# A DiT block on one core: a gate moved into the S5 readout, the widest pooling sums beside the chunk states, and stores spread over two queues

## The chip, the core and the metric

The kernel runs on one core of one Trainium2 chip. The metric is the device time of one execution in microseconds. Engines are named as the profile names them: PE is TensorE (matmuls), DVE is VectorE, ACT is ScalarE, SP is SyncE, which only issues DMAs here. ACT also issues DMAs from its own queue (ACTq).

## The reference

One layer over 1024 latent tokens of width 1024, with 256 context tokens that seed the scans. Cut to what matters:

```
sh1, sc1, g1, sh2, sc2, g2 = split(silu(c) @ w_mod + b_mod, 6)
h  = rms_norm(x, norm1_g) * (1 + sc1) + sh1
hc = (the same of ctx, modulated from c_ctx)
u_a, u_b, gate_a, gate_b = split(h @ w_in)         # 512, 512, 1024, 1024 columns
st_f, st_b = s5_states(u_a, both directions, seeded with the last state of hc @ w_in)
y   = gelu(real(c_f @ st_f + c_b @ st_b) + d_skip * u_a)
y_a = (y * sigmoid(y @ w_glu + b_glu)) @ w_branch_a
y_b = concat_j((mean over a window of 2, 4, 8, 16 in a row of 64 - u_b) @ pool_w[j]) * pool_scale @ w_branch_b
x   = x + g1 * ((sigmoid(gate_a) * y_a + sigmoid(gate_b) * y_b) @ w_out)
h2  = rms_norm(x, norm2_g) * (1 + sc2) + sh2
x   = x + g2 * ((silu(h2 @ w_gate) * (h2 @ w_up)) @ w_ffn_out)
out = rms_norm(x, final_norm_g)
```

## The kernel before, in words

Every product of float32 numbers is made in three passes (`mm3`, lines 264, 266 and 268): both operands are split into a rounded high part (`hi`) and a rest (`lo`), and hi·hi, hi·lo and lo·hi are summed in PSUM. ACT makes the high part of a weight tile (line 97), DVE the rest (line 98); `W8.take(ahead)` hands out the next tile and prepares as many behind it as `ahead` says, in the order of `weight_order`. Activations lie as 8 tiles of 128 features by 1024 tokens; one projection of 128 output columns (`proj`) is 8 k-steps of 6 matmuls of 128x512, so 48.

The kernel sets its own order: each engine runs its instructions in the order in which the code writes them, and a queue that waits holds all that stands behind it. Generators called `side` put other work between the k-steps of a projection. The stages:

- `startup`: c through w_mod (`mod_rows` multiplies two 512 KB `wm` tiles, which `load_mod` loads on SP), norm of x, transposes (`trans`), and the first three pooling columns (`mm`, into `self.ub`).
- `input_proj`: six projections. Beside them `build_e` makes the matrices E (16 steps, `ET`), `build_f` the matrices F (16 steps: DVE makes a tile `ef` in three operations, it is stored as `Fd`, and eight small matmuls with it give `kb`, stored as `Md`), and `pool_diff` the pooling branch of the windows j = 0 to 3: running sums by doubling (line 860), times the inverse width (line 867), minus the input (line 870), stored as `dT[j]`.
- `chunk_states`: U and ET tiles are loaded, and ET·U (line 1214) gives the states `V[0]` and `V[1]` of both directions, d = 0 and 1. Ahead of these products stands the gate b1. Then `scan_steps` on DVE (lines 1258 to 1261) beside the gates b2 to b7 and a0 to a3.
- readout: `f_phase(m)`, m = 0 to 3, 96 matmuls of 128x128 each (lines 1339 and 1341) with the loads `Fw`, `M` and `U` of `f_loads`; ACT applies gelu (line 1343) into `y`, and eight DMAs store it as `yT`. A gate is one projection with a sigmoid (line 1316), stored as `siga` or `sigb`.
- `late_gates`: the gates a4 to a7; between their k-steps the `yT` and `dT` tiles come back and are split (`tiles`), and w_mod's other sections are multiplied (`sections`). `pool_mm` applies pool_w. `branches`: four glu products, then both branches; output projection, FFN.

Of the kernel before, what the change touches and what calls it, by code (L numbers as in the profile page):

```python
# [11 lines left out]
F32 = mybir.dt.float32  # L12
# [223 lines left out]
class Kernel:  # L236
# [81 lines left out]
    def run(self):  # L318
# [36 lines left out]
        with self.pool("fpool", side="right") as fp:  # L355
            loads = [self.f_loads(fp, m) for m in range(2)]
            self.gate("a", 0, 4, side)
            for _ in side:
                pass
            for m in range(4):  # L360
                self.f_phase(fp, m, loads)
        par.close()
# [12 lines left out]
    def weight_order(self):  # L375
        W = self.W8 = Weights(self)
        cols = lambda w, c, n: w[:, c:c + n].rearrange("(k p) m -> p k m", p=128)
        two = [(0, 0), (0, 128)]
        w_in = self.w_in[0]
        W.units += W.job([cols(w_in, 896, 128)], 8, 128, [(0, 0)])  # L380
        for c in list(range(0, 512, 256)) + list(range(2048, 3072, 256)) + list(range(1024, 2048, 256)):
            W.units += W.job([cols(w_in, c, 256)], 8, 256, two)
            if c == 1280:
                W.units += W.job([self.pool_w[0].rearrange("j c m -> c j m")], 4, 128, [(0, 0)])
# [89 lines left out]
    def startup(self, hs):  # L474
# [168 lines left out]
        mm(0, 0)  # L643
        mm(1, 0)
# [9 lines left out]
        mod_rows(1)  # L654
        load_mod(2, 0)
        load_mod(2, 1)
# [96 lines left out]
    def input_proj(self):  # L753
# [6 lines left out]
        pools = [self.pool_diff(sp, j) for j in range(4)]  # L760
# [11 lines left out]
        def pool_steps():  # L772
            for j in range(4):
                next(pools[j])
                yield
                if 1 <= j <= 2:
                    begin(j + 1, self.ub[j + 1])
                yield from pools[j]

        pooling = pool_steps()  # L780
        for kt, q in ((6, 1), (7, 0), (7, 1)):
            self.mm_ub(kt, q)
            next(mats)
            self.drain(5)
# [27 lines left out]
        self.ub.append(self.proj(None, side))  # L812
# [9 lines left out]
        self.gate("b", 0, 1, side)  # L822
# [19 lines left out]
    def pool_diff(self, ep, j):  # L842
# [5 lines left out]
        up = ep.tile([128, 80, 16], F32, name="up", bufs=2)  # L848
# [7 lines left out]
        while True:  # L856
            a, b = (1, 0) if width == 2 else (width // 4, width // 4)
            s = ep.tile([128, 80, 16], F32, name="s", bufs=3)
            n = hi - b - lo - a
            G.tensor_tensor(s[:, lo + a:lo + a + n], cur[:, lo:lo + n], cur[:, lo + a + b:lo + a + b + n], op=OP.add)  # L860
            cur, lo, hi = s, lo + a, hi - b
            yield
            if width == w:
                break
            width *= 2
        d = cur[:, 8:72]
        G.tensor_tensor(d, d, self.inv[:, j, :, None].to_broadcast([128, 64, 16]), op=OP.mult)
        yield
        dn = ep.tile([128, 80, 16], F32, name="s", bufs=3)[:, 0:64].rearrange("p r s -> p (r s)")
        G.tensor_tensor(dn.rearrange("p (t b i) -> p i t b", t=8, b=16), d.rearrange("p (i t) b -> p i t b", t=8),  # L870
                        up[:, 8:72].rearrange("p (i t) b -> p i t b", t=8), op=OP.subtract)
# [314 lines left out]
    def chunk_states(self, es):  # L1186
# [21 lines left out]
        self.gate("b", 1, 2)  # L1208
# [121 lines left out]
    def f_phase(self, fp, m, loads):  # L1330
        nc = self.nc
        Fw, M, U = loads[m]
        y = fp.tile([128, 8, 128], F32, name="y")
# [13 lines left out]
        for t in range(8):  # L1347
            nc.sync.dma_start(self.yT[m][:, t].rearrange("(g c) n -> c g n", c=16), y[t * 16:t * 16 + 16])
# [95 lines left out]
    def late_gates(self):  # L1444
# [5 lines left out]
        def tiles():  # L1450

            srcs = []
            for kind, j in todo:
                for q in range(2):
                    srcs.append((kind, j, q, self.dT[j][:, q * 512:q * 512 + 512] if kind == "d" else
                                 self.yT[j][:, q * 4:q * 4 + 4].rearrange("p t n -> p (t n)")))
# [21 lines left out]
        def side(n, m):  # L1478
            for i in range(8):
                if i % 2 == 0 and i // 2 < n:  # L1480
                    next(tiles, None)
                elif m > 3 or i > 5:
                    next(sections, None)
# [11 lines left out]
    def branch(self, acts, left, side=None):  # L1495
        wh, wl = self.W8.take(min(2, left))
        ps = [self.psum() for _ in range(2)]
        for k in range(4):
            self.mm3(ps, wh[:, k], wl[:, k], acts[k], k == 0, k == 3)
            if side and k % 2:  # L1500
# [3 lines left out]
    def branches(self):  # L1504
        nc = self.nc

        ya = []
        for m in range(4):
            ps = self.branch(self.ys, 2, self.sections)
            ts = []  # L1510
            for q in range(2):
                t, u = self.ld(), self.ld()
                nc.scalar.activation(t, ps[q], AF.Sigmoid, bias=self.cols[:, 84 + m:85 + m])
                hi, lo = self.ys[m][q]
                nc.vector.tensor_tensor(u, hi.bitcast(F32), lo.bitcast(F32), op=OP.add)
                nc.vector.tensor_tensor(t, t, u, op=OP.mult)
                ts.append(t)
# [585 lines left out]
```

## Time and profile before

| what | value |
| --- | --- |
| median of 3 runs | 1316.56 us (1312.87 to 1317.75) |
| profiled execution | 1315.17 us, its span 1313.4 us |
| PE busy | 1246.1 us (95%) |
| DVE busy | 948.5 us (72%) |
| ACT busy | 531.4 us (40%) |
| mean granted clock of PE | 0.988 of full speed |
| HBM traffic | 182 GB/s over the span |

Times in the trace count from the start of the span. Busy time is that of the engine's instructions; idle time is put down to what ended it. `<-` reads "written from" in a row's names and "released by" in its brackets. The granted clock is a share of full speed: 0.50 is the lower of TensorE's two levels, 1.2 GHz, 1.00 the upper, 2.4 GHz.

### The profile page before, as it was taken

To read this page: it belongs to the slowest core of one execution; us is meant where nothing else is said; L and a number is where in the kernel's file an instruction comes from. 1 tells how busy PE (TensorE), PEld (TensorE's weight loads), DVE (VectorE), ACT (ScalarE), POOL (GpSimd) and SP (SyncE) were. 2 spreads that over 40 slices of the span, in tenths; PEclk is the share of its full clock that TensorE was granted. 3 is DMA by queue.
4 is the path that set the end of the run, shared out by engine and by line. 5 is a ranking of instruction groups with operands and counts; after the bars stand their busy time and mean duration, and the time that the engine had idled before them with its cause. 6 is when DMAs were issued, how large, how long until landed. Compare 5 with 4: busy or idle time off the path is not lost.

```text
span 1313.4 us, 16704 instructions
## 1 busy us (share of the span) xinstructions
PE 1246.1 (95%) x5811; PEld 1005.1 (77%) x5811; DVE 948.5 (72%) x1778; ACT 531.4 (40%) x951; POOL 13.4 (1%) x36
## 2 busy tenths in 40 slices
PE   6888989999969999999999999999999999999996
PEld 4567757878868788788887788888888888888884
DVE  7779983899606696855679977678778766578576
ACT  5564214742225521222574333333333345454443
POOL 4000000000000000000000000000000000000000
PEclk8999999999989999999999999999999999999998
DMA  8624569126477665653514733676666539776543
GB/s 286 182 97 162 180 184 339 65 81 216 145 183 251 208 211 189 209 175 111 199 35 141 235 107 108 147 233 206 227 209 203 175 126 321 272 227 194 189 144 129
DMA packets 196428, 239.79 MB, mean 183 GB/s; under 512 B 16928, under 2 KB 117880, under 8 KB 195832
## 3 DMA queue, kind: packets, MB, share of 16 engines
q1 hardware_dynamic: 188200, 222.92, 52.8%
q10 hardware_dynamic: 8144, 15.80, 3.2%
q8 instruction: 46, 0.75, 0.2%
q14 instruction: 38, 0.31, 0.1%
HBM read 168.67 MB, written 70.00 MB: 182 GB/s over the span
## 4 chain that ended last, share of the span: by engine, by line
PE 59%; DVE 19%; DMA 9%; ACT 7%; issue 4%; SPq 1%; ACTq 0%; DVEq 0%
PE ps L1724 10%; PE ps L1722 10%; PE ps L1723 9%; PE ps L1953 5%; PE ps L1954 5%; PE ps L1952 5%; PE ps L268 2%; PE ps L264 2%; PE ps L266 2%; PE ps L1568 2%; PE ps L1566 2%; PE ps L1567 2%; DMA wm<-in_w_mod_dram 1%; DVE wt L98 1%; DMA Md<-kb 1%
## 5 line engine op out<-in xcount | busy, mean ns | idle before, releaser
L1722 PE MATMUL ps<-a,wt 128*128 128x512 f32 x436 | 172.7, 396 | 2.4 <-ACT ld L1836 2.4
L1724 PE MATMUL ps<-a,wt 128*128 128x512 f32 x436 | 171.5, 393 | 0.3 <-DVE wt L124 0.3
L1723 PE MATMUL ps<-a,wt 128*128 128x512 f32 x436 | 170.6, 391 | 0.0
L124 DVE TENSOR_TENSOR a<-a,a 128x512 fp32r<-128x512 f32 x162 | 103.3, 685 | 30.9 <-ACT a L225 30.2
L1953 PE MATMUL ps<-a,a 128*128 128x512 f32 x308 | 122.0, 396 | 1.1 <-DVE a L124 1.1
L1952 PE MATMUL ps<-a,a 128*128 128x512 f32 x308 | 121.8, 396 | 0.0
L1954 PE MATMUL ps<-a,a 128*128 128x512 f32 x308 | 121.8, 396 | 0.0
L264 PE MATMUL ps<-h,wt 128*128 128x512 f32 x336 | 109.0, 405 | 5.1 <-ACT wt L97 4.7
L268 PE MATMUL ps<-h,wt 128*128 128x512 f32 x336 | 105.4, 395 | 2.0 <-DVE wt L98 1.9
L266 PE MATMUL ps<-h,wt 128*128 128x512 f32 x336 | 105.0, 394 | 0.0
L225 ACT ACTIVATE a<-a 128x512 fp32r<-128x512 f32 x154 | 87.1, 624 | 42.9 <-DVE a L124 13.2
L1722 PEld LDWEIGHTS ps<-a,wt 128*128 128x128 f32 x436 | 81.8, 188 | 21.1 <-ACT ld L1836 3.3
L1724 PEld LDWEIGHTS ps<-a,wt 128*128 128x128 f32 x436 | 81.9, 188 | 20.4 <-DVE wt L124 1.2
L1723 PEld LDWEIGHTS ps<-a,wt 128*128 128x128 f32 x436 | 82.0, 188 | 18.4
L1366 ACT ACTIVATE a<-ld 128x512 fp32r<-128x512 f32 x64 | 39.3, 629 | 128.4 <-DVE ld L1543 64.9
L264 PEld LDWEIGHTS ps<-h,wt 128*128 128x128 f32 x336 | 60.3, 190 | 19.9 <-ACT wt L97 5.7
L268 PEld LDWEIGHTS ps<-h,wt 128*128 128x128 f32 x336 | 60.8, 189 | 16.6 <-DVE wt L98 4.6
L266 PEld LDWEIGHTS ps<-h,wt 128*128 128x128 f32 x336 | 61.7, 190 | 12.5
L98 DVE TENSOR_TENSOR wt<-raw,wt 128x1024 fp32r<-128x1024 f32 (+1 forms) x42 | 39.8, 951 | 43.5 <-ACT wt L97 43.4
L1953 PEld LDWEIGHTS ps<-a,a 128*128 128x128 f32 x308 | 57.9, 188 | 15.8 <-DVE a L124 1.9
L1952 PEld LDWEIGHTS ps<-a,a 128*128 128x128 f32 x308 | 57.9, 188 | 14.0
L1954 PEld LDWEIGHTS ps<-a,a 128*128 128x128 f32 x308 | 57.9, 188 | 13.9
(336 smaller groups left out, 2456.0 us busy)
## 6 DMA issues: line engine op xcount, KB each, us to landing
raw<-in_w_ffn_in_dram SPq DMA_DIRECT2D x44, 512.0 KB
ld<-in_w_mod_dram SPq DMA_DIRECT2D x64, 256.0 KB
a<-in_w_ffn_out_dram SPq DMA_DIRECT2D x55, 256.0 KB
raw<-in_w_in_dram SPq DMA_DIRECT2D x10, 1024.0 KB
wm<-in_w_mod_dram SPq DMA_DIRECT2D x16, 512.0 KB
ld<-in_w_ffn_out_dram SPq DMA_DIRECT2D x22, 256.0 KB
x<-in_x_dram SPq DMA_DIRECT2D x8, 512.0 KB
ETd<-out ACTq DMA_DIRECT2D x16, 256.0 KB
```

Source lines behind the costliest of these rows:

```text
L98: nc.vector.tensor_tensor(lo, src, hi.bitcast(F32), op=OP.subtract)
L124: self.K.nc.vector.tensor_tensor(lo, self.src, hi.bitcast(F32), op=OP.subtract)
L225: K.nc.scalar.activation(hi, t, AF.Copy)
L264: nc.tensor.matmul(o, wh, ah, start=first, stop=False)
L266: nc.tensor.matmul(o, wh, al, start=False, stop=False)
L268: nc.tensor.matmul(o, wl, ah, start=False, stop=last)
L1722: nc.tensor.matmul(p, wh, ah, start=first and k == 0, stop=False, skip_group_check=on)
L1723: nc.tensor.matmul(p, wh, al, start=False, stop=False, skip_group_check=on)
L1724: nc.tensor.matmul(p, wl, ah, start=False, stop=last and k == 3, skip_group_check=on)
L1952: nc.tensor.matmul(p, ah[:, s], wh, start=first and i == 0, stop=False, skip_group_check=on)
L1953: nc.tensor.matmul(p, ah[:, s], wl, start=False, stop=False, skip_group_check=on)
L1954: nc.tensor.matmul(p, al[:, s], wh, start=False, stop=i == NB - 1, skip_group_check=on)
```

## The change

1. `run`: gate a4 stands between `f_phase` 1 and 2 of the readout; `late_gates` keeps a5 to a7, with five `tiles` and three `sections` beside each, and the fourth `pool_mm` stands behind them. The order of weight tiles follows.
2. `startup`: `mod_rows(1)` and the two `load_mod` behind it stand between `mm(0, 0)` and `mm(1, 0)` rather than behind `mm(0, 1)`.
3. `input_proj`: gate b0 first, in place of the column for pool j = 3 (896), gate b1 last; only three pools.
4. `pool_diff`: one operation makes sum·(1/w) - u, and two small ones on the first and last eight columns put the edges right.
5. `build_f`: `Fd` is stored by ACT's queue; six `ef` buffers rather than four, three `kb` rather than two.
6. `chunk_states`: the projection of pool j = 3 stands where gate b1 stood, and its sums run on DVE in the room of `V[1]`.
7. `f_phase`: `y` lies in three parts of `work`, used in turn, and its eight stores alternate between ACT and SP.
8. `branches`: y is loaded again from `yT` where DVE added its two parts (line 1515), and four `sections` steps stand beside a glu product, not two.

```diff
@@ run
             for m in range(4):
                 self.f_phase(fp, m, loads)
+                if m == 1:
+                    self.gate("a", 4, 5, None, 2)
@@ startup
         mm(0, 0)
+        mod_rows(1)
+        load_mod(2, 0)
+        load_mod(2, 1)
         mm(1, 0)
...
         mm(0, 1)
-        mod_rows(1)
-        load_mod(2, 0)
-        load_mod(2, 1)
         self.s5_load_b()
@@ input_proj
             self.mm_ub(kt, q)
+            self.drain(8)
             next(mats)
-            self.drain(5)
...
-        self.ub.append(self.proj(None, side))
+        self.gate("b", 0, 1, side)
         for m in range(4):
             ps = self.proj(hc, side)
...
-        self.gate("b", 0, 1, side)
+        self.gate("b", 1, 2, side)
@@ pool_diff
-        d = cur[:, 8:72]
-        G.tensor_tensor(d, d, self.inv[:, j, :, None].to_broadcast([128, 64, 16]), op=OP.mult)
+        dn = new_s()[:, 0:64].rearrange("p r s -> p (r s)")
+        d, u = (x[:, 8:72].rearrange("p (i t) b -> p i t b", t=8) for x in (cur, up))
+        o = dn.rearrange("p (t b i) -> p i t b", t=8, b=16)
+        G.scalar_tensor_tensor(o, d, 1.0 / w, u, op0=OP.mult, op1=OP.subtract)
         yield
-        dn = ep.tile([128, 80, 16], F32, name="s", bufs=3)[:, 0:64].rearrange("p r s -> p (r s)")
-        G.tensor_tensor(dn.rearrange("p (t b i) -> p i t b", t=8, b=16), d.rearrange("p (i t) b -> p i t b", t=8),
-                        up[:, 8:72].rearrange("p (i t) b -> p i t b", t=8), op=OP.subtract)
+
+        d, u, o = (x[:, ::7] for x in (d, u, o))
+        inv = self.inv[:, j].rearrange("p (i t) -> p i t", t=8)[:, ::7]
+        G.tensor_tensor(d, d, inv[:, :, :, None].to_broadcast([128, 2, 8, 16]), op=OP.mult)
+        G.tensor_tensor(o, d, u, op=OP.subtract)
         nc.sync.dma_start(self.dT[j], dn)
@@ ef_tiles
-        return sp.tile([128, 576], F32, name="ef", bufs=4), sp.tile([128, 576], F32, name="eft", bufs=2)
+        return sp.tile([128, 576], F32, name="ef", bufs=6), sp.tile([128, 576], F32, name="eft", bufs=2)
@@ build_f
-                    kb[u] = sp.tile([128, 240], F32, name="kb", bufs=2)
+                    kb[u] = sp.tile([128, 240], F32, name="kb", bufs=3)
...
-                nc.sync.dma_start(self.Fd[bu // 2][:, bd, bu % 2 * 4:bu % 2 * 4 + 4],
+                nc.scalar.dma_start(self.Fd[bu // 2][:, bd, bu % 2 * 4:bu % 2 * 4 + 4],
@@ chunk_states
-        self.gate("b", 1, 2)
+
+        room = V[1].rearrange("p i g b -> p (i g b)")
+        part = [room[:, i * 1280:i * 1280 + 1280].rearrange("p (r b) -> p r b", b=16) for i in (0, 1, 2, 3, 1, 2)]
+        wide = self.pool_diff(3, lambda: part.pop(0), lambda: part.pop(0))
+        next(wide)
+        wide.send(self.proj(None))
+        for _ in wide:
+            pass
@@ f_phase
-        y = fp.tile([128, 8, 128], F32, name="y")
+        y = self.work.rearrange("p a q -> p (a q)")[:, m % 3 * 1024:m % 3 * 1024 + 1024].rearrange(
+            "p (g n) -> p g n", g=8)
...
-            nc.sync.dma_start(self.yT[m][:, t].rearrange("(g c) n -> c g n", c=16), y[t * 16:t * 16 + 16])
+            (nc.scalar if t % 2 else nc.sync).dma_start(
+                self.yT[m][:, t].rearrange("(g c) n -> c g n", c=16), y[t * 16:t * 16 + 16])
@@ late_gates
-        for m in range(4, 8):
-            self.gate("a", m, m + 1, side(4, m))
-            pool_mm(m - 4)
+        for m in range(5, 8):
+            self.gate("a", m, m + 1, side(), 3 if m == 7 else 1)
+            pool_mm(m - 5)
+        for _ in tiles:
+            pass
+        pool_mm(3)
@@ branches
+        us = [self.ld(self.y_half(0, q)) for q in range(2)]
         for m in range(4):
             ps = self.branch(self.ys, 2, self.sections)
             ts = []
             for q in range(2):
-                t, u = self.ld(), self.ld()
+                t, u = self.ld(), us[q]
                 nc.scalar.activation(t, ps[q], AF.Sigmoid, bias=self.cols[:, 84 + m:85 + m])
-                hi, lo = self.ys[m][q]
-                nc.vector.tensor_tensor(u, hi.bitcast(F32), lo.bitcast(F32), op=OP.add)
                 nc.vector.tensor_tensor(t, t, u, op=OP.mult)
+                if m < 3:
+                    us[q] = self.ld(self.y_half(m + 1, q))
+                next(self.sections, None)
                 ts.append(t)
```

Three pieces of the engines' orders show what moves. The first is PE's, at the end of the second readout group (m = 1), before; the U tile with the lower number is that of the second group, the other that of the third.

```order
L1339 MATMUL ps<-U_2998,M 128x128
L1341 MATMUL ps<-V_2191,Fw 128x128
L1341 MATMUL ps<-V_2192,Fw 128x128
L1339 MATMUL ps<-U_3322,M 128x128
L1341 MATMUL ps<-V_2191,Fw 128x128
L1341 MATMUL ps<-V_2192,Fw 128x128
```

And the same place of the changed kernel, where lines 1358 and 1360 are the readout's two products.

```order
L1358 MATMUL ps<-U_2998,M 128x128
L1360 MATMUL ps<-V_2185,Fw 128x128
L1360 MATMUL ps<-V_2186,Fw 128x128
L264 MATMUL ps<-h_270,wt 128x512 x2
L266 MATMUL ps<-h_271,wt 128x512 x2
L268 MATMUL ps<-h_270,wt 128x512 x2
L264 MATMUL ps<-h_270,wt 128x512 x2
L266 MATMUL ps<-h_271,wt 128x512 x2
L268 MATMUL ps<-h_270,wt 128x512 x2
```

Behind the second group stand the 48 matmuls of gate a4, on h and a weight tile, before the third begins.

The second is SP's queue from the loads for the third group to the first tiles of the late gates, before.

```order
L1322 DMA Fw<-Fd_82 128x2048
L1324 DMA M<-Md_86 128x4x256
L1327 DMA U_3322<-uT_70 128x8x128
L1348 DMA yT_88<-y 16x8x128 x8
L1322 DMA Fw<-Fd_83 128x2048
L1324 DMA M<-Md_87 128x4x256
L1327 DMA U_3365<-uT_71 128x8x128
L1348 DMA yT_89<-y 16x8x128 x8
L1348 DMA yT_90<-y 16x8x128 x8
L1348 DMA yT_91<-y 16x8x128 x8
L1360 DMA ld<-dT_92 128x512 x2
```

In the changed kernel it begins with the weight tiles of the gate behind.

```order
L79 DMA raw<-in_w_in_dram 128x8x256
L79 DMA raw<-in_pool_w_dram 128x4x128
L1340 DMA Fw<-Fd_82 128x2048
L1342 DMA M<-Md_86 128x4x256
L1345 DMA U_3320<-uT_70 128x8x128
L1367 DMA yT_88<-work 16x8x128 x4
L1340 DMA Fw<-Fd_83 128x2048
L1342 DMA M<-Md_87 128x4x256
L1345 DMA U_3362<-uT_71 128x8x128
L1367 DMA yT_89<-work 16x8x128 x4
L79 DMA raw<-in_w_in_dram 128x8x256
L79 DMA raw<-in_w_glu_dram 128x4x512
```

Four of eight yT stores have left this queue, and two weight loads have moved ahead of the third group's matrices, two more ahead of the third group's stores.

The third is DVE's, between the powers of the S5 matrices and the first steps of the scan in `chunk_states`, before.

```order
L1091 TENSOR_SCALAR AI<-AI,sgn 128x512
L1093 TENSOR_SCALAR AI<-AI 128x64
L98 TENSOR_TENSOR wt<-raw,wt 128x1024
L1258 TENSOR_TENSOR work<-V_2191,AR 128x640
L1259 TENSOR_TENSOR work<-work,AI 128x640
L1260 TENSOR_TENSOR V_2191<-V_2191,work 128x640
```

In the changed kernel line 1276 is the scan's first operation.

```order
L1104 TENSOR_SCALAR AI<-AI 128x64
L98 TENSOR_TENSOR wt<-raw,wt 128x1024
L856 MEMSET V_2186 128x128
L857 MEMSET V_2186 128x128
L867 TENSOR_TENSOR V_2186<-V_2186 128x1264
L867 TENSOR_TENSOR V_2186<-V_2186 128x1232
L867 TENSOR_TENSOR V_2186<-V_2186 128x1168
L867 TENSOR_TENSOR V_2186<-V_2186 128x1040
L876 SCALAR_TENSOR_TENSOR V_2186<-V_2186 128x8x128
L881 TENSOR_TENSOR V_2186<-V_2186,inv 128x2x128
L882 TENSOR_TENSOR V_2186<-V_2186 128x2x128
L1276 TENSOR_TENSOR work<-V_2185,AR 128x640
```

The nine operations of pool j = 3, in the room of `V[1]`, have come between the weight's rest and the scan.

## Rows read from the trace of the kernel before

**Rows 1.** TensorE's waits, whole span: what it waited for, us in total, times, longest.
```profile
PE ps L1339 <- DMA U<-uT: 6.5, 2, 3.7
PE ps L264 <- ACT wt L97: 6.5, 4, 4.2
...
PE ps L1171 <- DVE kb L1140: 4.0, 3, 1.7
PE ps L1171 <- DVE ef L1159: 3.5, 3, 1.9
PE ps L543 <- DMA wm<-in_w_mod_dram: 3.5, 2, 3.0
```

**Rows 2.** Stretches: length, busy PE PEld DVE ACT POOL (x instructions), clock, DMA share, GB/s.
```profile
52.90:56.30 3.40, 3.40 (x9) 2.63 (x10) 2.15 (x7) 0.57 (x1) 0.00 (x0) 0.50 0.36 62
93.00:137.00 44.00, 36.13 (x191) 29.20 (x191) 43.41 (x70) 20.34 (x38) 0.00 (x0) 0.96 0.42 151
162.00:196.00 34.00, 26.68 (x183) 19.54 (x182) 30.25 (x46) 4.56 (x16) 0.00 (x0) 1.00 0.62 192
196.00:230.00 34.00, 30.77 (x168) 26.20 (x167) 10.44 (x28) 14.07 (x37) 0.00 (x0) 1.00 1.03 337
373.70:380.60 6.90, 6.21 (x29) 6.24 (x30) 0.00 (x0) 2.02 (x2) 0.00 (x0) 0.51 0.34 66
387.40:390.80 3.40, 3.40 (x9) 2.61 (x9) 0.93 (x1) 0.00 (x0) 0.00 (x0) 0.50 0.92 141
443.00:466.00 23.00, 21.39 (x94) 17.23 (x93) 20.32 (x32) 12.33 (x21) 0.00 (x0) 1.00 0.41 141
```

**Rows 3.** Timeline, TensorE, startup: start us, us, line, operation, count, [idle before <-releaser].
```profile
38.49 1.92 PE L543 MATMUL ps<-wm,ccols 128*32 128x512 f32 x16
...
51.74 1.07 PE L543 MATMUL ps<-wm,ccols 128*32 128x512 f32 x8 [2.95 <-DMA wm<-in_w_mod_dram]
```

**Rows 4.** Timeline of SyncE's queue, startup.
```profile
39.18 2.03 SPq L494 DMA_DIRECT2D wm<-in_w_mod_dram  x4
```

**Rows 5.** VectorE by line, 86 to 205 us: count, busy, mean ns, idle before.
```profile
L1155 DVE TENSOR_TENSOR ef<-Pr,cparts 128x576 f32<-128x576 f32 x16 | 12.0, 752 | 3.2 <-DMA Fd<-ef 3.2
...
L870 DVE TENSOR_TENSOR s<-s,up 128x1024 f32<-128x1024 f32 x4 | 8.7, 2167 | 0.0
...
L860 DVE TENSOR_TENSOR s<-s 128x1232 f32<-128x1232 f32 (+2 forms) x6 | 8.2, 1359 | 0.0
...
L867 DVE TENSOR_TENSOR s<-s,inv 128x1024 f32<-128x1024 f32 x4 | 4.9, 1218 | 0.0
```

**Rows 6.** Tile Fd, its stores: ns least, median, most; first and last start.
```profile
L1166 SPq DMA_DIRECT2D Fd<-ef x16: 360/844/1854, 141.8 to 202.3; - x16
```

**Rows 7.** Chain that ended last, 150 to 170 us: start, us, what.
```profile
158.29 6.89 DMA Fd<-ef
```

**Rows 8.** Timeline of ScalarE and its queue, start of the readout.
```profile
353.03 0.33 ACTq L1317 DMA_DIRECT2D siga<-tmp  x1
353.39 1.28 ACT L1343 ACT_TABLE_LOAD   x1 [0.39 <-ACT tmp L1316]
...
367.27 2.03 ACT L1343 ACTIVATE y<-ps 128x512 f32<-128x512 f32 x2 [9.24 <-DMA yT<-y]
```

**Rows 9.** Timeline of VectorE, first operation of the scan.
```profile
229.87 0.82 DVE L1258 TENSOR_TENSOR work<-V,AR 128x640 f32<-128x640 f32 x1 [18.82 <-ACT V L1220]
```

**Rows 10.** Timeline of TensorE, chunk states.
```profile
216.51 2.33 PE L1214 MATMUL ps<-U,ET 128*128 128x160 f32 x16
...
226.89 11.11 PE L1214 MATMUL ps<-U,ET 128*128 128x160 f32 x80 [1.68 <-DMA ET<-ETd]
```

**Rows 11.** Timeline of TensorE, third and fourth readout group.
```profile
365.10 0.46 PE L1339 MATMUL ps<-U,M 128*128 128x128 f32 x2 [2.84 <-DMA U<-uT]
...
374.39 0.77 PE L1339 MATMUL ps<-U,M 128*128 128x128 f32 x2 [3.70 <-DMA U<-uT]
```

**Rows 12.** Timeline of SyncE's queue, readout.
```profile
358.39 6.89 SPq L1348 DMA_DIRECT2D yT<-y  x8
```

More of the change, by code (lines that the diff above doesn't have):

```diff
@@ L379, in weight_order @@
         w_in = self.w_in[0]
-        W.units += W.job([cols(w_in, 896, 128)], 8, 128, [(0, 0)])
-        for c in list(range(0, 512, 256)) + list(range(2048, 3072, 256)) + list(range(1024, 2048, 256)):
+        one = lambda c: W.job([cols(w_in, c, 128)], 8, 128, [(0, 0)])
+        W.units += one(2048)
+        for c in list(range(0, 512, 256)) + list(range(2304, 3072, 256)) + list(range(1024, 2048, 256)):
             W.units += W.job([cols(w_in, c, 256)], 8, 256, two)
-            if c == 1280:
-                W.units += W.job([self.pool_w[0].rearrange("j c m -> c j m")], 4, 128, [(0, 0)])
+            if c == 256:
+                W.units += one(2176)
+                W.units += one(896)
+            if c == 1536:
+                W.units[-1:-1] = W.job([self.pool_w[0].rearrange("j c m -> c j m")], 4, 128, [(0, 0)])
         W.units += W.job([cols(self.w_glu[0], 0, 512)], 4, 512, [(0, i * 128) for i in range(4)])
@@ L759, in input_proj @@
         hc = [sp.tile([128, 8, 256], F32R, name=f"hc{i}") for i in range(2)]
-        pools = [self.pool_diff(sp, j) for j in range(4)]
+        pools = [self.pool_diff(j, lambda: sp.tile([128, 80, 16], F32, name="up", bufs=2),
+                                lambda: sp.tile([128, 80, 16], F32, name="s", bufs=3)) for j in range(3)]
         def begin(j, ps):
@@ L772, in pool_steps @@
         def pool_steps():
-            for j in range(4):
+            for j in range(3):
                 next(pools[j])
                 yield
-                if 1 <= j <= 2:
-                    begin(j + 1, self.ub[j + 1])
+                if j == 1:
+                    begin(2, self.ub[2])
                 yield from pools[j]
@@ L840, in proj, with pool_diff @@
         return ps
-    def pool_diff(self, ep, j):
+    def pool_diff(self, j, new_up, new_s):
         nc = self.nc
@@ L847, in pool_diff @@
         ps = yield
-        up = ep.tile([128, 80, 16], F32, name="up", bufs=2)
+        up = new_up()
         nc.vector.memset(up[:, 0:8], 0.0)
@@ L857, in pool_diff @@
             a, b = (1, 0) if width == 2 else (width // 4, width // 4)
-            s = ep.tile([128, 80, 16], F32, name="s", bufs=3)
+            s = new_s()
             n = hi - b - lo - a
@@ L1347, in f_phase, with y_half @@
         for t in range(8):
-            nc.sync.dma_start(self.yT[m][:, t].rearrange("(g c) n -> c g n", c=16), y[t * 16:t * 16 + 16])
+            (nc.scalar if t % 2 else nc.sync).dma_start(
+                self.yT[m][:, t].rearrange("(g c) n -> c g n", c=16), y[t * 16:t * 16 + 16])
+    def y_half(self, m, q):
+        return self.yT[m][:, q * 4:q * 4 + 4].rearrange("p t n -> p (t n)")
     def at1(self, dt=F32R):
@@ L1455, in tiles @@
                     srcs.append((kind, j, q, self.dT[j][:, q * 512:q * 512 + 512] if kind == "d" else
-                                 self.yT[j][:, q * 4:q * 4 + 4].rearrange("p t n -> p (t n)")))
+                                 self.y_half(j, q)))
             got = [self.ld(srcs[i][3]) for i in range(3)]
@@ L1476, in late_gates, with side @@
         sections = self.mod_sections((2, 3, 4))
-        def side(n, m):
+        def side():
             for i in range(8):
-                if i % 2 == 0 and i // 2 < n:
+                if i % 2 == 0 or i == 7:
                     next(tiles, None)
-                elif m > 3 or i > 5:
+                else:
                     next(sections, None)
@@ L1499, in branch @@
             self.mm3(ps, wh[:, k], wl[:, k], acts[k], k == 0, k == 3)
-            if side and k % 2:
+            for _ in range(k % 2 if side else 0):
                 next(side, None)
```

## The prediction

> **What bounds the kernel now.** I read the list of TensorE's waits first: its few long lines say where time can come from at all. The reader should see three places [rows 1]: U tiles of the readout (6.5 us in two waits) with the weight copy behind them (one wait of 4.2), the F matrices (4.0 on kb and 3.5 on ef), and the wm rows of the startup (3.5). Next came busy time by stretch, with the granted clock [rows 2]. Two things are to be seen there. In 162 to 196 us VectorE is busy 30.25 of 34 us and TensorE 26.68, so the F build is paced by VectorE. And each of the three idle places is followed by a stretch at the lower clock level (0.50 of full speed, so 1.2 GHz): 52.9 to 56.3, 373.7 to 380.6, 387.4 to 390.8. TensorE had just waited each time, so a stall costs its length and half of the busy time in the slow stretch behind it. TensorE's work stays the same in amount, so only the removal of idle or half-speed time can shorten the span. The profiled execution took 1315.17 us, 1.4 less than the median of 1316.56; the sum is made against it and the 1.4 added back.
>
> **Startup.** Sixteen matmuls on the second wm pair (1.92 us) go from behind two groups of projections to between them [rows 3]. Their wm buffers come free that much earlier, and so do the four loads that reuse them: issued from 39.18, needed by the matmuls that start at 51.74 after a wait [rows 3, 4], so up to 12.6 us from issue to use. Moved behind the first projection group the issue comes at about 34, some 5 us earlier, and the data at about 46.5, while TensorE asked for the first eight of these matmuls at about 47.7 (51.74 less the wait of 2.95 and the 1.07 of the eight) and for the others at 48.8 [rows 3]. The four loads pass the slab and S5 loads in SyncE's queue, which so come some 2 us later (2.03 for four issues [rows 4]); the DMA is free enough to make that up (share 0.36 in 52.9 to 56.3 [rows 2]). The waits (3.5) go, and with them the slow stretch (3.4 us, half of it lost: 1.7). Against it: the sixteen matmuls may run at the lower level, 1.92 more at worst; of which the idle time before the following projections takes most, as I estimate. I take 5.0; the ends are 2 (loads come in time for the first half only) and 6.
>
> **F build.** Pool j=3 leaves this stretch for the next: three adds at 1.36 and a slightly longer first one (together 5.5), a scaling at 1.22 and a subtraction at 2.17 [rows 5], 8.9 us of VectorE. That leaves 30.25 - 8.9 = 21.4 against TensorE's 26.68 [rows 2], so TensorE becomes the bound and its 4.0 + 3.5 = 7.5 us of waiting [rows 1] has no cause left, provided F stores land. VectorE waited 3.2 us for them [rows 5]; with six ef buffers instead of four, two more F (over 3 us each: 16 stores lie between 141.8 and 202.3 [rows 6]) pass before a buffer is needed, which covers the 6.89 us to landing seen on the chain [rows 7]. The stores leave SyncE, where one holds the queue 0.84 us in the median [rows 6], and Md stores and weight loads queue behind it; on ScalarE an issue took 0.33 [rows 8], and kb copies, context evictions and weight copies are what is queued behind it. ScalarE is busy 4.56 of these 34 us [rows 2], so 11 issues at 0.33 to 0.84 fit. The other pools trade 1.22 + 2.17 for one operation with both steps and two small ones on a quarter of the elements (0.3 to 0.4 each, estimated from the 1.22). The trace has no such fused operation: it is bounded by the 1.22 below and 2.17 above, and I take 2.17, since its strided access is that of the subtraction. That saves 0.4 each, 0.5 for those that stand where VectorE is full (43.41 of 44 us in 93 to 137 [rows 2]). Term 8.0; ends 4 (stores still late) and 12 (some of the 7.9 us that TensorE idles in 93 to 137 goes too).
>
> The Trainium skill ("DMA: Bandwidth & Descriptors", section "Issuing engines are not separate DMA queues") says that DMAs interleave on the same 16 engines whichever engine starts them, and that several issuers save only sequencer time. By that rule the move itself is worth 0.84 - 0.33 us an issue and the landing of 6.89 stays; were the landing the pace, the sum would be 20.0 with this term at 1.0 in place of 27.0 with it at 8.0, which is the second rival below.
>
> **Chunk states.** The pooling projection stands where gate b1 stood, of the same length, so the ET products begin as before. Pool j=3 then runs on VectorE while it had 18.82 us of idleness [rows 9]: two evictions (2.0 for two in the readout [rows 8]), 5.5 of adds, 2.2 and 0.8, from 216.51 [rows 10] to about 227, before the scan's first operation at 229.87. Its cover is that idleness. What is late next are the four d=1 ET loads, queued on SyncE behind the store that waits for the pool. TensorE starts the last d=0 group at 226.89 [rows 10] and wants the first d=1 tile 2.2 us later, with DMA saturated up to there (share 1.03, 337 GB/s [rows 2]). A U load of the readout took some 7 us to its use; the bound from that is a loss of 5. Only the first of the four can cost much, since the others are wanted 2.2 us apart: I take a loss of 1.5, nearer to nothing, as the four loads of before cost 1.7 for the one at 226.89; ends 0 and 5.
>
> **Readout.** Before, the third and fourth readout groups find their U not there: its issue stands just before the yT stores of 358.39, its first use is at 365.10, 2.84 late, and that of the fourth at 374.39, 3.70 late [rows 11, 12]. Now 48 gate matmuls stand between the second and third group. Ninety-four such took 21.39 us in 443 to 466 [rows 2], so 48 last 10.9. The third group starts at 365.10 - 2.84 + 10.9 = 373.2, 8 us after its U came; the fourth 5.6 later (374.39 - 3.70 - 365.10) at 378.8, 4 after. SyncE issues four yT stores per group instead of eight (6.89 us in the queue before [rows 12]), so these loads come no later. The weight wait (4.2) fell on a copy that ScalarE made late; the new order issues that raw load before the third group's matrices, and the copy has the gate to hide behind; the gate's two sigmoids and two siga stores (0.33 each [rows 8]) are all that it adds to ScalarE beside. So 6.5 + 4.2 = 10.7 goes, and the two slow stretches (6.21 us busy, 3.1 lost; 3.4, 1.7 lost [rows 2]): 15.5. The next thing that can be late is the first d tile for the late gates: its load still stands behind the last yT stores, and a5 follows the readout as a4 did.
>
> ScalarE now switches function tables twice more, gelu to sigmoid and back, at 1.28 each, and stood idle 9.24 us between two evictions here for the landing of stores [rows 8]; with three y slots in place of one that wait goes and pays for 2.6. The ends are 9 (evictions held by stores, or the copies late) and 16.5.
>
> **Late gates and glu.** Three gates take five tiles each rather than four of four, and eight section tiles (256 KB each) go over to the glu products, as do eight reloads of y (256 KB) in place of eight adds. In 443 to 466 the DMA moved 141 GB/s, 3.2 MB [rows 2]; with 4 MB more it is 7.2 MB, 21.5 us at the 337 GB/s seen when saturated, against 22 us of matmuls. VectorE is even: eight adds out, eight section products in. I take 0; ends -4 and +2 (the late weight waits, 6.5 - 4.2 = 2.3).
>
> **Sum.** 5.0 + 8.0 - 1.5 + 15.5 + 0 = 27.0; 1315.2 - 27.0 = 1288.2, as a median 1289.6.
>
> **The rivals.**
> *The readout gains half.* ScalarE issues half of the yT stores, each of which may wait for an older transfer, U among them (at 365.10); the eviction behind it, the gate's sigmoids and the copies of weights come later. For it speaks the 9.24; against it three slots and 10.9 us of cover. At 7 of 15.5: 1298.
> *The F build stays with the DMA.* If landing, not issue or VectorE, sets the pace (the chain has 6.89 for one Fd), one of the 8.0 comes: 1296.6. Against it: waits on Fd were 3.2 of VectorE's 34.
> *The glu products wait for DMA*, 4 to 6 us, as worked out: 1294 to 1296.
> *More than forecast:* 6 to 8 of the 7.9 us in 93 to 137 go as well: 1282 to 1284.
> *Slower:* a store issued on ScalarE holds that engine until it has landed. Then an F costs 6.9 + 0.5 us of own work there (4.56 in 34, nine F) against TensorE's 3.3 (60.5 us less 7.5, by 16): 16 x 4.1 = 65, so 1355. It decides from some 2.8 us held per store, and makes the whole slower by 0.5% from 4.9 (27.0 + 6.6 = 34 us over 16 F). Against it: the issue of siga took 0.33, and the table load behind it began 0.36 after it [rows 8].
> *The change doesn't do what it says:* each stall moves to the next late transfer, 1310 to 1317.
>
> **How the numbers follow.** Forecast 0.50 (1283 to 1294), readout half 0.15, F build 0.15, glu 0.08, more 0.05, nothing 0.04, slower 0.03. 1279 to 1302 leaves out the last two and the joint case of two partial ones, some 0.1 to 0.15 together. About 0.5%, 6.6 us, can be told from no change: faster means below 1310, and only the last two cases lie above: 0.93, 0.04, 0.03.
>
> **What would show it.** Right: no wait on wm at about 47 us and full clock behind it; in the F stretch TensorE without idle time and VectorE at about 0.8 (21.4 of 26.7); in the readout the gate's matmuls between the second and third group, and no U wait, full clock from 350 to 400. A wait on ET of 1 to 2 us may be seen near 229. Wrong: TensorE waits on kb or ef with ScalarE's queue as the late one; y evictions waiting on stores; ld or u tiles late at 430 to 460; the scan's last step after 351.4, where the readout must begin.

## The result

The changed kernel takes 1301.99 us (1299.87 to 1305.00, 4 runs) against 1317.15 (1312.87 to 1321.20) before: ratio 0.9885, interval 0.9862 to 0.9907. That is 15.2 us faster where 27.0 were forecast, at the upper edge of the stated 1279 to 1302. Its profiled execution took 1299.87 us, span 1298.1.

TensorE's waits after the change come first (what it waited for, us in total, times, longest).

```profile
PE ps L1128 <- DVE ef L1123: 6.3, 5, 2.4
PE ps L1232 <- DMA ET<-ETd: 5.7, 1, 5.7
PE ps L264 <- ACT wt L97: 3.6, 4, 2.0
PE ps L268 <- DVE wt L98: 3.5, 3, 2.6
...
PE ps L264 <- ACT a L1390: 2.3, 2, 1.3
...
PE ps L549 <- DMA wm<-in_w_mod_dram: 0.5, 1, 0.5
...
PE ps L1182 <- DVE ef L1170: 0.3, 1, 0.3
```

Before, two of these read:

```profile
PE ps L1117 <- DVE ef L1112: 4.9, 3, 2.4
...
PE ps L1214 <- DMA ET<-ETd: 3.2, 3, 1.7
```

The waits of [rows 1] that the forecast went by are gone or short: U and kb have no row, the F matrices 0.3, wm 0.5, and the weight copies fell from 6.5 to 3.6. What was waited for on ET in three pieces is now one wait of 5.7 us. New, with 2.3 us, are waits on the tiles of the late gates (a, line 1390). The longest row, on `ef` in the E build, grew from 4.9 to 6.3; the forecast had no term for it. Busy time by stretch (columns as in [rows 2]) shows where these lie:

```profile
150.00:184.00 34.00, 33.70 (x229) 24.93 (x229) 28.93 (x52) 7.34 (x24) 0.00 (x0) 1.00 0.98 290
185.00:204.00 19.00, 19.00 (x85) 15.70 (x85) 9.90 (x26) 2.59 (x6) 0.00 (x0) 1.00 0.99 325
...
385.00:395.00 10.00, 7.89 (x32) 5.98 (x33) 7.34 (x11) 5.87 (x9) 0.00 (x0) 1.00 0.95 317
395.00:405.00 10.00, 9.00 (x39) 6.81 (x38) 3.95 (x7) 6.86 (x11) 0.00 (x0) 1.00 0.36 122
...
415.00:425.00 10.00, 7.39 (x31) 5.01 (x29) 7.32 (x12) 8.17 (x15) 0.00 (x0) 1.00 0.42 146
445.00:455.00 10.00, 7.96 (x28) 6.40 (x29) 9.79 (x17) 4.20 (x7) 0.00 (x0) 0.83 0.88 305
```

In the F build (150 to 184) TensorE is now busy 33.70 of 34 us. In the late gates and glu products TensorE loses one to three us in each of the four ten-us stretches shown between 385 and 455; before, it idled only 3.3 us in all from the end of gate a4 (399.75) to the output projection (555.19).

By when the same instruction starts in the two traces:

| up to | before | after | gain of the stage | forecast |
| --- | --- | --- | --- | --- |
| last pooling column of the startup | 89.16 | 84.27 | 4.9 | 5.0 |
| first product of ET and U | 216.51 | 203.89 | 7.7 | 8.0 |
| last product of ET and U | 237.70 | 229.06 | -4.0 | -1.5 |
| first readout product | 351.38 | 341.41 | 1.3 | 0 |
| first product of the output projection | 555.19 | 538.93 | 6.3 | 15.5 + 0 |
| last FFN product | 1302.37 | 1287.15 | -1.0 | 0 |

The readout itself did as forecast. The first gate matmul behind it, before and after:

```profile
387.13 1.01 PE L264 MATMUL ps<-h,wt 128*128 128x512 f32 x2 [4.19 <-ACT wt L97]
```

```profile
373.68 0.71 PE L264 MATMUL ps<-h,wt 128*128 128x512 f32 x2
```

From the first readout product to it were 35.7 us (351.38 to 387.13) and are 32.3 (341.41 to 373.68) with 10.9 of gate a4 inside: 14.4 less, and the slow stretch behind (1.7) is gone too. The 6.3 of that row mean that some 9.8 were lost again between 374 and 539. From the first matmul behind gate a4 and the readout to the output projection TensorE took 155.4 us before and takes 165.3; 5.6 of the difference is idle time, the rest the same matmuls taking longer.

### The profile page after: what moved, and what is told of

Its sections match the earlier page's. It is cut to its first block, busy times and chain, and to the rows that moved or that the text cites. A ratio compares the mean times of both kernels' runs of the same rounds, so it can differ in the third digit from the quotient of the medians.

```text
span 1298.1 us, 16710 instructions
## 1 busy us (share of the span) xinstructions
PE 1244.7 (96%) x5811; PEld 1002.0 (77%) x5811; DVE 942.4 (73%) x1774; ACT 534.8 (41%) x953; POOL 13.4 (1%) x36
## 4 chain that ended last, share of the span: by engine, by line
PE 65%; DVE 18%; ACT 6%; DMA 5%; issue 3%; SPq 1%; ACTq 0%; DVEq 0%
PE ps L1751 10%; PE ps L1753 10%; PE ps L1752 10%; PE ps L1982 5%; PE ps L1983 5%; PE ps L1981 5%; PE ps L264 4%; PE ps L268 4%; PE ps L266 4%; PE ps L1595 2%; PE ps L1597 2%; PE ps L1596 2%; DVE wt L98 1%; DMA yT<-work 1%; DVE V L1278 1%
## 5 line engine op out<-in xcount | busy, mean ns | idle before, releaser
L1391 DVE TENSOR_TENSOR a<-ld,a 128x512 fp32r<-128x512 f32 x64 | 43.1, 690 | 44.5 <-ACT a L1390 43.7
```

The costliest lines, as they stand in the source:

```text
L1391: self.nc.vector.tensor_tensor(lo, src, hi.bitcast(F32), op=OP.subtract)
```

## The experiments

All edits but one are to the changed kernel; times are medians, and each ratio is to the kernel before on the same chip. A run of the changed kernel unedited beside three of them gave 1301.55 (0.9894, 0.9874 to 0.9914).

> The changed kernel itself, unedited, as the measure for the three beside it: 1299 to 1304 us.

### The loss between the two directions of the chunk products

The rows of the changed kernel: TensorE, then SyncE's queue.

```profile
203.89 8.86 PE L1232 MATMUL ps<-U,ET 128*128 128x160 f32 x64
218.44 10.92 PE L1232 MATMUL ps<-U,ET 128*128 128x160 f32 x64 [5.69 <-DMA ET<-ETd]
```

```profile
213.82 0.33 SPq L883 DMA_DIRECT2D dT<-V  x1
214.25 2.20 SPq L1211 DMA_DIRECT2D ET<-ETd  x4
```

The four loads go out right behind the store, 4.2 us before the second half of the products can start. First the store was moved to ScalarE's queue:

```diff
-        nc.sync.dma_start(self.dT[j], dn)
+        (nc.scalar if j == 3 else nc.sync).dma_start(self.dT[j], dn)
```

> One edit to the changed kernel: the store of dT[3] goes out on ScalarE's queue, so the four d=1 ET loads have no store ahead of them in SyncE's queue. Theory (queue order): in the changed kernel these loads are issued at 214.25 us, behind the store of 213.82, while their buffers come free from 206 to 212.5 on; the loads now go out then, TensorE's wait of 5.7 us on ET falls under 1 and the half-speed stretch behind it goes, so 5 to 7 us off the changed kernel's 1302. Rival (the data path): the loads take as long whenever they are issued, or V[1] is held by the pool's sums and its store, so that d=1 products wait for their evictions; the wait moves and the time stays within 1.5 us of the changed kernel.

1298.64 (0.9857, 0.9824 to 0.9891); its trace matches that of the changed kernel at every stage within 2 us. The wait stays, at 4.8 us, on an eviction. ScalarE's rows tell why:

```profile
213.42 0.33 ACTq L883 DMA_DIRECT2D dT<-V  x1
213.80 0.49 ACT L1236 ACTIVATE V<-ps 128x384 f32<-128x384 f32 x1 [9.21 <-DVE V L882]
```

The store is written ahead of the products, so ScalarE stood for 9.21 us, until VectorE had made what is to be stored, before its first eviction: my edit put the hold on another queue. (A hold is a time in which an engine or a queue stands on one instruction while others wait behind it.) The same fault is in the next run, where the result of pool j=3 lies in a weight tile, its store stays on ScalarE, and raw weights go by GpSimd's queue (as in the section on the late gates):

```diff
+        part[5] = self.wt().bitcast(F32).rearrange("p (r b) -> p r b", b=16)
```

> Three edits to the changed kernel: raw weights of the late gates by GpSimd's queue; the result of pool j=3 goes into a weight tile instead of the room in V[1]; its store goes out on ScalarE's queue. Theory (two causes at the chunk states: the ET loads queue behind the store, and V[1] is held until the store has landed): with both taken away TensorE's wait of 4.8 to 5.7 us between the two directions falls under 1.5 and the slow stretch behind it goes; 4 to 7 us faster than 1296.9. Rival (the scan on VectorE, which begins no earlier, takes up the time in the gates beside it): the wait goes, weight copies are waited for instead, within 2 us of 1296.9.

1297.55 (0.9850, 0.9827 to 0.9872): no gain over 1296.9, and the wait is there with 4.9 us, so freeing V[1] did not help while ScalarE was held. Last, with the store on SyncE and written behind the loads, the result still in a weight tile:

```diff
-        for _ in wide:
-            pass
+        for _ in range(5):
+            next(wide)
...
             if d == 0:
+                for _ in wide:
+                    pass
                 side = self.scan_steps()
```

> Edits to the changed kernel: raw weights of the late gates by GpSimd's queue; the result of pool j=3 goes into a weight tile, and its store stays on SyncE but is written behind the four d=1 ET loads. Theory (queue order alone held the products: first SyncE's, and in the run with the store on ScalarE that engine's, which stood on the store ahead of all evictions): TensorE's wait between the two directions falls from 5.7 us to under 1.5, the slow stretch behind it goes, and 4 to 7 us come off 1296.9. Rival (the scan on VectorE, which starts no earlier, or the late gates take the time up again): the wait goes, and the time stays within 2 us of 1296.9.

1291.28 (0.9815, 0.9782 to 0.9848), 5.6 us under the run with raw loads alone. All 128 products run in one row, and the wait is gone:

```profile
203.33 17.55 PE L1233 MATMUL ps<-U,ET 128*128 128x160 f32 x128
```

So the order of the queues made this loss. Whether the room in V[1] would have held the products next is not shown, since no run left the result there and moved only the store behind the loads.

### What the gate's place is worth

```diff
-                if m == 1:
+                if m == 3:
                     self.gate("a", 4, 5, None, 2)
```

> One edit to the changed kernel: gate a4 stands behind the fourth readout group again, not between the second and third; all else stays, the orders of weights and late gates too. Theory (the readout term was right and part of it was handed on): the two waits on U return (5 to 7 us, and 3 to 5 us of half speed behind them), while the 2.3 us that the first pooling product waits for its d tiles go, since a gate covers them again: 5 to 9 us slower than the changed kernel. Rival (the gate only moves the waits): the stalls in the late gates shrink by as much as the readout loses, so within 2 us of the changed kernel.

1299.33 (0.9869, 0.9838 to 0.9899): not slower, so my theory fell in this form. Waits of the third and fourth group returned, and those of the late gates went, for about the same sum, 7.7 us against 8.7 (TensorE, 330 to 560 us):

```profile
PE ps L1358 <- DMA yT<-work: 5.3, 2, 3.8
PE ps L268 <- DVE wt L98: 2.4, 1, 2.4
```

The gate was set back twice more, beside kernels in which holds of the late gates had been taken away: first the raw loads, then also the pool's store and the yT stores (both below).

> Two edits to the changed kernel: raw weights of the late gates by GpSimd's queue, and gate a4 behind the fourth readout group again. Beside the run with the first edit alone (1296.9) it prices the gate's place once the loop through SyncE's queue is cut. Theory (the readout's gain was real and was given back to the loop): with the loop cut the place counts, so this is 3 to 8 us slower than 1296.9. Rival (the late gates take up any gain of the readout, loop or not, since their tiles come at their own pace): within 2 us of 1296.9.

1299.38 (0.9867, 0.9846 to 0.9888) against 1296.89: 2.5 us by the medians, 1.3 by the ratios, not told apart from nothing.

> To the kernel of 1284.8 (raw weights and the last two groups' yT stores by GpSimd's queue, pool j=3 stored behind the ET loads): gate a4 stands behind the fourth readout group again. Theory (with the holds of the late gates gone the readout's gain counts in full): the U waits and the slow stretches behind them return and nothing takes them up, 6 to 12 us slower than 1284.8. Rival (the late gates take it up even so): 2 to 3 us slower, as with the raw loads alone moved.

1295.62 (0.9827, 0.9799 to 0.9855) against 1284.79 (0.9753, 0.9733 to 0.9774): 10.8 us by the medians, 9.7 by the ratios. The waits of the readout are back, and nothing takes them up (TensorE, 330 to 560 us):

```profile
PE ps L1361 <- DMA U<-uT: 3.6, 1, 3.6
...
PE ps L1361 <- DMA yT<-work: 1.8, 1, 1.8
```

The same edit costs nothing that can be told beside the first two kernels and some 10 us beside the third, by what stands behind it.

### What took the gain in the late gates

Rows of the changed kernel: ScalarE, SyncE's queue, TensorE.

```profile
371.16 6.92 ACTq L1367 DMA_DIRECT2D yT<-work  x4
378.20 2.11 ACT L1362 ACTIVATE work<-ps 128x512 f32<-128x512 f32 x2 [7.08 <-DMA yT<-work]
...
385.48 0.63 ACT L1390 ACTIVATE a<-ld 128x512 fp32r<-128x512 f32 x1 [5.17 <-DMA ld<-dT]
...
410.82 0.63 ACT L1390 ACTIVATE a<-ld 128x512 fp32r<-128x512 f32 x1 [6.75 <-DMA ld<-yT]
```

```profile
371.15 11.07 SPq L1367 DMA_DIRECT2D yT<-work  x8
382.61 2.73 SPq L1384 DMA_DIRECT2D ld<-dT  x6
...
393.26 0.99 SPq L1384 DMA_DIRECT2D ld<-dT  x2
403.79 0.38 SPq L79 DMA_DIRECT2D raw<-in_w_branch_b_dram  x1
```

```profile
386.16 0.51 PE L264 MATMUL ps<-a,wt 128*128 128x512 f32 x1 [1.32 <-ACT a L1390]
...
418.81 0.74 PE L264 MATMUL ps<-a,wt 128*128 128x512 f32 x2 [1.95 <-ACT wt L97]
...
447.04 0.73 PE L268 MATMUL ps<-a,wt 128*128 128x512 f32 x2 [2.65 <-DVE wt L98]
```

Two holds can be read. The fourth group's products end at 373.9, but ScalarE evicts them at 378.20, since it is issuing its four yT stores of the third group until then; the last stores and, behind them, the first d loads (382.61) follow, and gate a5 is over before its pooling product has tiles. And SyncE issues no load from 394.3 to 403.8, because a raw load waits there for the buffer of a weight that is not yet split, with the next y tiles behind it; ScalarE then waits 6.75 for one of them, ahead of the next weight copy. The second hold was cut first:

```diff
-            self.K.nc.sync.dma_start(v[:, s], src)
+            (self.K.nc.gpsimd if getattr(self.K, 'late_raw', 0) else self.K.nc.sync).dma_start(v[:, s], src)
```

> One edit to the changed kernel: from the late gates on, the loads of raw weights are issued by GpSimd's queue instead of SyncE's. Theory (a loop through SyncE's queue): a raw load waits in SyncE's queue until VectorE has made the rest of the weight before it, all tile loads stand behind it (no load from 394.3 to 403.8 us), the y tiles then come 6 us later still, ScalarE waits for them ahead of the gate's sigmoids and the next weight copy; with raw loads off that queue the tiles flow, ScalarE's waits of 10.1 us on yT fall under 4, and 4 to 8 us of TensorE's waits in the late gates go. Rival (the DMA itself, or the eight ld buffers): tiles come as late as before, within 1.5 us of the changed kernel.

1296.89 (0.9857, 0.9831 to 0.9882), 4.7 us faster than 1301.55; ScalarE's waits on yT from 370 to 425 us fell from 10.3 in the unedited run beside it to this:

```profile
ACT a L1390 <- DMA ld<-yT: 6.0, 2, 3.0
```

The same edit to the kernel before:

> One edit to the kernel before: from the late gates on, raw weights are loaded by GpSimd's queue. Theory (before, TensorE entered the late gates late enough, behind its own stalls, and the loop was hidden): within 2 us of 1317. Rival (the raw loads in SyncE's queue cost the same in any order): 3 to 5 us faster than before, as in the changed kernel.

1313.88 (0.9984, 0.9970 to 0.9997), 0.4 to 4 us faster; by the ratios that is 2.1 us, under half of the gain in the changed kernel. So this hold was not wholly hidden in the old order, and how much of the 4.7 us is due to the new one stays open. Then the first hold, by giving the last y its own place:

```diff
+        halves = [y[:, 0:4], y[:, 4:8]] if m < 3 else [
+            self.tmp().rearrange("p (g n) -> p g n", g=4) for _ in range(2)]
...
+                next(stores, None)
```

> One edit to the changed kernel: the fourth y goes into two tiles of its own (one for each half) and its stores, 16 half-sized ones on SyncE, are issued one at each k-step of gates a5 and a6 rather than ahead of the loads of the first d tiles. Theory (late tiles): the d loads go out 3 to 5 us earlier than 382.6, the first pooling product no longer waits (2.3 us), and the later waits of the late gates (6 us on weight copies and tiles) shrink too: 2 to 6 us off. Rival (SyncE's queue and the eight ld buffers set the pace there, not the first loads): the first waits go and come back within the three gates, within 1.5 us of the changed kernel.

1301.12 (0.9877, 0.9848 to 0.9907), nothing. With the raw loads moved as well, and with that and the pool's store:

> Two edits to the changed kernel, each measured alone: raw weights of the late gates by GpSimd's queue (1296.9) and the last y stored step by step beside gates a5 and a6 (1301.1, against 1301.6 unedited). Theory (two holds one behind the other: the late first tiles, and the loop through SyncE's queue, which took up what earlier tiles gave): together 2 to 4 us faster than 1296.9, since the first pooling product's waits of 3 us and the slow stretch behind them are now really lost time. Rival (a third hold further on takes it up): within 1.5 us of 1296.9.

> The edits of the two runs beside it together. Theory: what they gain adds up, 1296.9 less 4 to 7 and less 2 to 4, so 1286 to 1291. Rival (the glu stage, with VectorE at 0.95 and the sections' loads, sets the time from there on): 1293 or more.

1297.84 (0.9858, 0.9829 to 0.9887) and 1290.73 (0.9807, 0.9777 to 0.9838), nothing beyond 1296.89 and 1291.28. The d loads did go out at 375.97, but the edit takes two of three tmp tiles, for which ScalarE then waited ahead of gate a5's and a6's work (rows of the run of 1297.84):

```profile
395.05 0.60 ACT L1334 ACTIVATE tmp<-ps 128x512 f32<-128x512 f32 x1 [5.32 <-DMA siga<-tmp]
...
413.01 0.69 ACT L1509 ACTIVATE tmp<-ps,cols 128x512 f32<-128x512 f32 x1 [4.65 <-DMA siga<-tmp]
```

So these three runs said nothing on the hold. It was taken away without that cost, on top of 1291.28:

```diff
-            (nc.scalar if t % 2 else nc.sync).dma_start(
+            (nc.gpsimd if m > 1 else nc.scalar if t % 2 else nc.sync).dma_start(
```

> To the kernel of 1291.3 (raw weights by GpSimd's queue, pool j=3 in a weight tile and stored behind the ET loads): the 16 yT stores of the third and fourth readout group go out on GpSimd's queue. Theory (stores on ScalarE hold the fourth group's evictions, 7 us, and through them the last stores and the first d loads): these evictions follow their products at once, the d loads go out 4 us or more earlier, and the first pooling product's two waits (3.8 us) and the slow stretch behind them go: 3 to 6 us off. Rival (the next hold in the late gates takes it up, as it did with the last y stored step by step): within 1.5 us of 1291.3.

1284.79 (0.9753, 0.9733 to 0.9774), 6.5 us less by the medians, 8.2 by the ratios. ScalarE evicts the fourth group as its products end, and SyncE's d loads go out at 367.30:

```profile
364.85 1.11 ACT L1365 ACTIVATE work<-ps 128x512 f32<-128x512 f32 x1 [0.50 <-PE ps L1363]
367.53 1.21 ACT L1365 ACTIVATE work<-ps 128x512 f32<-128x512 f32 x1 [1.57 <-PE ps L1363]
```

TensorE's wait on these tiles is 0.3 us in 330 to 560, and from gate a5 to the output projection it now takes 157.2 us (367.25 to 524.47), against 165.3 in the changed kernel and 155.4 for the same work before. Last, four tiles per gate instead of five, alone and with it:

```diff
-                if i % 2 == 0 or i == 7:
+                if i % 2 == 0:
```

> To the kernel of 1291.3: a late gate has four tiles and four section steps beside it, as before the change, not five and three; the two tiles left over follow gate a7. Theory (the fifth tile stands on ScalarE ahead of the gate's sigmoids and of the next weight copy, and waits there for its load): ScalarE's waits on yT ahead of the sigmoids go and 1 to 3 us of TensorE's waits with them. Rival (the load comes no earlier and is waited for elsewhere): within 1 us either way, or slower by the tiles behind a7.

> The edits of the two runs beside it together. Theory: both gains, 1282 to 1288. Rival (VectorE in the glu stage sets the time): 1290 or more.

1289.40 (0.9792, 0.9769 to 0.9815) and 1286.02 (0.9762, 0.9742 to 0.9781): 1.9 less and 1.2 more, neither told apart from nothing. No run shows that the number of tiles matters.

### The other terms

Fd stores back on SyncE (`nc.sync` in place of `nc.scalar` in `build_f`):

> One edit to the changed kernel: the 16 Fd stores go back to SyncE's queue; six ef buffers, the moved pool and the one-operation mean stay. Theory (VectorE's work set the pace of the F build, and its work was cut): 0 to 2 us slower than the changed kernel, TensorE's waits on ef and kb under 2 us. Rival (the queue set the pace): the waits of 7.5 us on ef and kb return for the most part, 5 to 8 us slower.

1301.04 (0.9878, 0.9848 to 0.9908); in the F build TensorE waits 0.2 us on ef and none on kb. The queue was worth nothing that the times show.

The additions of y's parts in place of the reloads:

> One edit to the changed kernel: the glu products take y from VectorE's additions of its two parts, as before the change, rather than from eight reloads of 256 KB; the four section steps per product stay. Theory (the reloads make the glu stage short of loads): the wait of 2.65 us on the weight's rest at 447 us, behind VectorE's wait for a section tile, and the half-speed stretch behind it go: 3 to 4 us faster than the changed kernel. Rival (VectorE, over 0.95 busy from 445 to 465, is the bound there): the eight additions of 0.69 come on top, 1 to 5 us slower.

1304.84 (0.9914, 0.9896 to 0.9933), 3.3 slower: the rival. In 430 to 470 us, changed kernel first, then this one, both under the columns of [rows 2]:

```profile
430.00:470.00 40.00, 37.02 (x152) 29.07 (x151) 34.55 (x54) 16.50 (x28) 0.00 (x0) 0.96 0.78 257
```

```profile
430.00:470.00 40.00, 33.48 (x129) 25.34 (x128) 36.01 (x57) 14.09 (x24) 0.00 (x0) 0.91 0.52 170
```

With less DMA (170 against 257 GB/s) and more VectorE work TensorE gets less done, which speaks for VectorE as the scarcer there.

The second wm pair back behind `mm(0, 1)`:

> One edit to the changed kernel: the second wm pair's matmuls and the two loads behind it stand where they stood before the change. Theory (the stall and its half-speed stretch are lost time that nothing later makes up): the wait of 3.0 us and the slow stretch return, 4 to 6 us slower than the changed kernel. Rival (a later place waits for loads or for VectorE anyway and takes up the difference): under 2 us slower.

1305.26 (0.9921, 0.9899 to 0.9944), 3.7 slower; in the trace the startup ends 2.3 later. But no wait on wm came back: these matmuls follow without a gap at 49.49. What differs from the changed kernel is a slow group at 36.44 (granted clock 0.60 from 36.4 to 40, against 1.00):

```profile
24.04 1.83 PE L572 MATMUL ps<-ident,x 128*128 128x128 f32 x6 [3.60 <-DVE x L537]
...
36.44 3.64 PE L585 MATMUL ps<-h,wt 128*128 128x512 f32 x9 [1.09 <-ACT h L477]
...
49.49 2.00 PE L549 MATMUL ps<-wm,ccols 128*32 128x512 f32 x16
```

The wait of 3.60 for x at 24 is not the edit's: the two runs above (Fd stores and additions), with the startup of the changed kernel, have 3.53 and 3.40 there, and reach the startup's last group of matmuls at 77.74 and 77.96, where this run reaches it at 80.57. So the size of the startup term is borne out in part, its mechanism is not; what else of the change moved the startup stays open.

## Why the prediction was wrong

**The step that failed is the term of the late gates and glu ("I take 0; ends -4 and +2").** It cost some 9.8 us. The readout term of 15.5 was right where it stood (14.4 and 1.7), and the prediction even named what would be late next, the first d tile, but priced it at nothing with the words that its load stands behind the last yT stores and a5 follows the readout "as a4 did". It did not. Before, a4 began 4.2 us late and ran its first 3.4 us at the lower clock level, and SyncE's queue reads:

```profile
389.98 3.07 SPq L1360 DMA_DIRECT2D ld<-dT  x5
```

So these loads had 9.8 us until the first pooling product, at 399.75. In the new order they go out at 382.61, 7.4 us earlier, but TensorE is ready for that product at 384.84, 14.9 us earlier: its stalls are gone, while the tiles stayed tied to ScalarE's stores and SyncE's queue.

The runs with the gate set back (nothing, nothing clear of noise, and some 10 us) show that the stall was handed on, and the runs on the two holds show to what: 4.7 us to raw loads in SyncE's queue, 6.5 to the yT stores of the last two groups in ScalarE's and SyncE's queues, which no run parted. Together that is more than the 9.8, and part of the first stood in the old order too. With both taken away the stretch is within 2 us of its length before (157.2 against 155.4). What the yT stores cost in the old order was not measured. The rival "the readout gains half" had the right engine (stores that hold evictions) and a time only 4 us off (1298), but looked for it in the readout itself; there it was hidden, and it came out one stage later. The last rival, that each stall moves to the next late transfer, is what became of a part of the readout's gain, but it gave 1310 to 1317.

**Chunk states: mechanism right, size off.** The loads queued behind the store cost 4.0, not 1.5. The prediction let the products wait for loads before as well (the wait of 1.68 at 226.89 [rows 10]) and so took only part of the lateness. In the new order the first four groups had their tiles at once (8.86 us without a gap), so the whole lateness of the d=1 loads was uncovered, 5.69 us; before, 3.2 us of waiting on ET were spread over three groups.

**F build: right.** 7.7 for 8.0; the fused operation took 2174 ns (2.17 taken), the two small ones 418 and 657 (0.3 to 0.4 each), so that the trade saved 0.1 us a pool and not 0.4, and Fd issues on ScalarE 0.37. With the Fd stores back on SyncE nothing changes, so the queue was worth nothing, and the VectorE work (with the buffers, which were not undone) was the term. The Trainium skill ("DMA: Bandwidth & Descriptors", "Issuing engines are not separate DMA queues"), by which another issuer saves little, agrees with that run. The rival drawn from it, that landing sets the pace, did not come: VectorE has no wait on Fd left.

**Startup: size right (4.9 for 5.0), mechanism not shown.** The loads into the freed wm buffers do go out earlier (32.20 instead of 39.18, about 34 taken) and the wait on wm is down to 0.5. But in the run that undid the move they go out at 39.36, and the wait does not come back.

**Glu as DMA's stage: not borne out.** With the additions in place of the reloads the kernel was 3.3 us slower. What the reloads cost by themselves no run shows.

## What to carry to other kernels

When a stall goes, price the next place that waits by the time at which its data come, not by how it stood before: the stall may have been what covered it. A store written into an engine's queue held everything behind it here until it could go out: the pool's store, where it stood on ScalarE, held that engine 9.21 us for VectorE's sums, and four yT stores held it 6.92 us while older yT stores landed. Moving a store to another busy engine's queue moves the hold, as the pool's store shows. Follow the first load of the next stage back through every queue to the last thing that it must wait for.

## What the runs showed that was not expected

GpSimd's queue, unused before, took whole weight loads and 16 of the yT stores, and the time fell by 4.7 and 6.5 us. With these two and the store behind the ET loads the kernel takes 1284.79 us, 17 under the changed kernel and 33 under the one before (0.9753). That is 4.8 us under the forecast for the change as it was.
